# The feed-forward output of a hybrid decoder layer in three chunks of rows, two of them by a seven-product block scheme

## The chip, the cores and the metric

The kernel runs on one core of one Trainium2 chip. The metric is the device time of one execution in microseconds (us), the median of several runs. All arithmetic is fp32 in value: TensorE multiplies in a reduced fp32 format, so every operand is split into a high and a low part, and each block product is three products (high by high, high by low, low by high).

## The reference

One step of a one-layer decoder: 512 prompt rows and 8 sample rows (520 columns of a transposed activation), model width 1024, hidden width 2816 = 22 blocks of 128.

```python
h = x + Mixer(rmsnorm(x))            # retention, dilated attention, gates, w_o
a, b = split(rmsnorm(h) @ w_ffn_in, 2)
h = h + (silu(a) * b) @ w_ffn_out    # (520 x 2816) @ (2816 x 1024)
y = rmsnorm(h)
```

Beside `y`, the retention states and the key and value rows of the mixer are outputs.

## The kernel before

Activations lie transposed: 128 features on the partitions, the 520 columns in two halves of 260 (256 prompt and 4 sample columns, `HF`). Weights come from one array `wall` in the order of their use, as 194 subs; a sub is 128x1024, eight tiles of 128x128. `load_sub` has SyncE's queue load one (four buffers `raw`). `split_sub` has ScalarE write the high part `wh` of a whole sub, and two steps later VectorE the low part `wl` and the queue the load of the sub that takes the freed buffer; both parts have three buffers. A `product` takes one weight tile and runs six matmuls of 260 columns, three for each half. A `unit` runs `nk` products into one PSUM tile `pm` (two banks, one for each half; two such tiles exist) and asks for splits two subs ahead at every eighth product.

The program writes the order of every engine by hand. After each product `pump` takes one step of a queue of generators (`P`, `S`, `Q`), which issue the work beside the weights: scores, sample states, norms. `drain("P")` steps the generators until none is left, with nothing between.

The stages are, by the time of the profile: retention with its projections to about 430 us, then the output projections, attention, gates and `w_o` to about 946 us, then the feed forward. Its input (L1100 to L1121) makes 22 hidden blocks `U`, each by two units of 8 products: VectorE scales `fa` and `fb` (L1105, L1111), ScalarE takes Silu, VectorE multiplies (L1112), and the result is split into a high part (L1113) and a low part (L1114). After all 22, the output (L1194) makes eight column blocks `c` of the result by a unit of 22 products each, and `ev_f` adds them onto `hT` (L1191). The eighth is made one half after the other (L1200).

The final norm works by column block and half: `fin_T` transposes the block on TensorE into two of three PSUM banks `sp` (L212, three transposes), `fin_sq` has ScalarE sum the squares (`junk`, L1142 and L1144), `fin_g` has VectorE scale it (`yt` L1148, `ys` L1150). I call these three together a finish; there are 16. `gen_final` spreads two finishes over ten steps. `fin_out` makes the norm of a half from all its finishes (a power on GpSimd, L221), scales and stores.

```python
    for c in range(7):
        unit(NFF, usrc, lambda pm, c=c: ev_f(pm, c))
        push("P", gen_final(c))
```

Of the kernel before, what the change touches and what calls it, by code (L numbers as in the profile page):

```python
# [22 lines left out]
NFF = 22  # L23
NSUB = 194
GAMMA = [1.0 - 2.0 ** (-5.0 - h) for h in range(RH)]


@with_exitstack
def tile_hybrid_layer(
# [35 lines left out]
    def f32(ap):  # L65
        return ap.bitcast(F32)
# [70 lines left out]

    raw, split = {}, {}

    NRAW = 4  # L140

    def load_sub(s):
# [3 lines left out]

    def split_sub(s):
        if s >= NSUB or s in split:
            return
        r = raw.pop(s)  # L150
        h = wpool.tile([128, 1024], F32R, tag="wh", name=f"wh{s}")
        l = wpool.tile([128, 1024], F32R, tag="wl", name=f"wl{s}")
        A.activation(h, r, AF.Copy)  # L153
        split[s] = (h, l)

        def low():
            V.tensor_tensor(l, r, f32(h), op=ALU.subtract)  # L157
            load_sub(s + NRAW)

        later(2, low)  # L160

    tr = rp.tile([128, 2, C], F32, name="tr")
# [19 lines left out]
    def product(pm, n, k, nk, src, fs):  # L182
        h, l = split[n // 8]
        j = n % 8
        wh, wl = h[:, j * 128:(j + 1) * 128], l[:, j * 128:(j + 1) * 128]
        xh, xl = src(k)
        for w, x, first, last in ((wh, xh, k == 0, False), (wh, xl, False, False), (wl, xh, False, k == nk - 1)):
            for f in fs:
                PE.matmul(pm[:, f, :HF], w, x[:, f * HF:(f + 1) * HF], start=first, stop=last)  # L189

    def unit(nk, src, evac=None):
        pm = pmain.tile([128, 2, 512], F32, tag="pm", name="pm")
        for k in range(nk):
            n = pos[0]
            pos[0] += 1
            if n % 8 == 0:
                for s in range(3):
                    split_sub(n // 8 + s)
            product(pm, n, k, nk, src, (0, 1))
            pump()  # L200
        if evac:
            evac(pm[:, :, :HF])
        return pm[:, :, :HF]

    def sbank(name="sp"):
# [40 lines left out]

    for s in range(2):
        split[s] = tuple(wpool.tile([128, 1024], F32R, tag=t, name=f"{t}{s}") for t in ("wh", "wl"))

    def w_split(s, i):  # L250
        q = slice(512 * i, 512 * i + 512)
        (h, l), r = split[s], raw[s]
        A.activation(h[:, q], r[:, q], AF.Copy)
        V.tensor_tensor(l[:, q], r[:, q], f32(h[:, q]), op=ALU.subtract)

# [9 lines left out]
    for s in range(2):  # L265
        raw.pop(s)
        load_sub(NRAW + s)

# [72 lines left out]
    for h in range(RH):  # L341
# [245 lines left out]
        for which in ("q", "k"):  # L587
            e0, e1 = rot(which)
            if h == 0 and which == "q":
# [3 lines left out]
                for u, k in [(u, k) for k in range(4) for u in range(2)] + [(u, k) for u in range(2) for k in range(4, 8)]:  # L593
                    product(pms[u], 8 * u + k, k, 8, src, (0, 1))
                    if u and k == 4:
                        split_sub(2)
                    pump()
                    if k == 7:
                        (e0, e1)[u](pms[u][:, :, :HF])
# [442 lines left out]
    rs2 = hp.tile([128, C], F32, name="rs2")  # L1042
    fp = open_pool("fp", "right")
    X2 = bpool.tile([128, 16, C], F32R, tag="bx", name="X2")
    acc2 = fp.tile([128, C], F32, name="acc2")
# [48 lines left out]
    push("P", gen_norm2())  # L1094
    U = [None] * (2 * NFF)
    UA = bpool.tile([128, 16, C], F32R, tag="bg", name="UA")
    UB = fp.tile([128, 28, C], F32R, name="UB")
    for i in range(2 * NFF):
        U[i] = UA[:, i, :] if i < 16 else UB[:, i - 16, :]
    for i in range(NFF):  # L1100
# [50 lines left out]

    def gen_final(c):
        for _ in range(5):
            yield
        a = fin_T(c, 0)
        yield
        fin_sq(c, 0, *a)
        fin_g(c, 0, *a)
        yield
        yield  # L1160
        b = fin_T(c, 1)
        yield
        fin_sq(c, 1, *b)
        fin_g(c, 1, *b)

    def fin_out(f, sp, sp2):
        fin_sq(7, f, sp, sp2)
        s = fp.tile([128, 4], F32, tag="fs", bufs=2, name="fs")
        V.tensor_reduce(s[:, 0:2], ssp[:, 2 * f:2 * f + 2, :], AX.X, ALU.add)
        r = rstd_rows(fp, s[:, 0:2], 128, 2, D, "nf")  # L1170
        fin_g(7, f, sp, sp2)
        V.tensor_reduce(s[:4, 2:3], sss[:, f, :], AX.X, ALU.add)
# [12 lines left out]
    def usrc(k):  # L1185
        return U[k], U[NFF + k]

    def ev_f(pm, c, f=None):
        fs = slice(None) if f is None else slice(f, f + 1)
        h = halves(hT[:, c, :])[:, fs]  # L1190
        V.tensor_tensor(h, pm[:, fs], h, op=ALU.add)  # L1191
# [63 lines left out]
def _layout(np, i):  # L1255
# [14 lines left out]
    ffo = [j for c in range(NFF) for j in (c, NFF + c)]  # L1270
    flat = np.concatenate([x.reshape(-1, 128, 128) for x in
                           (w_in[seq], _tiles(f["w_pa"][0]), w_in[seq2], _tiles(f["w_pb"][0]), _tiles(f["w_o"][0]), ff[ffo],
                            _tiles(f["w_ffn_out"][0]))])
    wall = np.ascontiguousarray(flat.reshape(NSUB, 8, 128, 128).transpose(0, 2, 1, 3)).reshape(NSUB, 128, 1024)
# [24 lines left out]
```

## Time and profile before

| what | value |
|---|---|
| median of 3 runs | 1331.48 us (1330.41 to 1332.78) |
| the profiled execution, its own time | 1332.56 us |
| its span, first to last instruction | 1330.8 us |
| TensorE matmul busy | 1304.4 us, 98%, x10681 |
| VectorE busy | 662.5 us, 50% |
| ScalarE busy | 476.7 us, 36% |
| mean granted TensorE clock | 0.991 |

PE is TensorE's matmuls, PEld its weight loads, DVE VectorE, ACT ScalarE, POOL GpSimd, SP SyncE (SPq its queue). L189 is the line of `kernel.py` with the matmul of `product`; L157 and L153 are the low and the high part of the weight split. A busy PE is not PE at its peak: one matmul of 260 columns is recorded with 0.28 us, but starts 0.12 us after the one before it. In a stage without waits the start-to-start time is the cost.

### The profile page before, as it was taken

Reading aid. Unit: us, or ns where it says so; the run is one execution under the profiler, and the core shown is the slowest. Engines: PE = TensorE matmul, PEld = TensorE weight load, DVE = VectorE, ACT = ScalarE, POOL = GpSimd, SP = SyncE. Lnnn points to the kernel's source line nnn. Section 1 sums busy time; section 2 is a strip of 40 time slices with the busy share of each in tenths; the row PEclk is TensorE's granted clock in tenths of the full one; section 3 lists DMA queues with packets and bytes.
Section 4 is the critical chain, followed back from the end, with each engine's and each line's share of the span. In section 5 each row is a group of like instructions: output and inputs, shape, how many; then the busy total and the mean of one; then the engine's idle time right before and its main releaser. Section 6 shows DMA issues by size and latency. Waiting matters only on the chain.

```text
span 1330.8 us, 25131 instructions
## 1 busy us (share of the span) xinstructions
PE 1304.4 (98%) x10681; PEld 1273.4 (96%) x10681; DVE 662.5 (50%) x1271; ACT 476.7 (36%) x828; POOL 83.0 (6%) x69
## 2 busy tenths in 40 slices
PE   8999999999989999999999999999999999999997
PEld 7899999898889999999999999899999999999997
DVE  7867536746655432233545454376444444443323
ACT  4554334534453421143434343233222222222222
POOL 3601001001002000000000000030000000000000
PEclk9999999999899999999999999999999999999999
DMA  6267235646475233435555455634223332333221
GB/s 216 84 227 231 89 114 206 228 129 230 157 255 189 80 96 95 135 115 160 156 159 164 134 171 175 217 104 136 82 94 96 96 90 86 95 112 96 80 64 66
DMA packets 89777, 183.33 MB, mean 138 GB/s; under 512 B 12024, under 2 KB 33944, under 8 KB 89664
## 3 DMA queue, kind: packets, MB, share of 16 engines
q1 hardware_dynamic: 88944, 180.64, 43.2%
q8 instruction: 84, 1.38, 0.4%
q10 hardware_dynamic: 720, 1.07, 0.2%
q14 instruction: 29, 0.24, 0.1%
HBM read 155.70 MB, written 25.98 MB: 137 GB/s over the span
## 4 chain that ended last, share of the span: by engine, by line
PE 89%; DVE 4%; DMA 3%; ACT 1%; issue 1%; POOL 1%; SPq 1%; POOLq 0%; DVEq 0%; ACTq 0%
PE pm L189 78%; PE sp L212 3%; PE sp L442 2%; DMA vb<-vd 2%; PE sp L460 2%; DVE wl L157 1%; PE sp L394 1%; PE sp L852 1%; PE sp L802 1%; PE oacc L555 1%; PE sacc L997 1%; PE sp L791 0%; ACT wh L153 0%; DMA xb<-xT 0%; DVE X L313 0%
## 5 line engine op out<-in xcount | busy, mean ns | idle before, releaser
L189 PE MATMUL pm<-X,wh 128*128 128x260 f32 x4608 | 756.6, 286 | 3.9 <-DVE X L244 3.6
L189 PEld LDWEIGHTS pm<-X,wh 128*128 128x128 f32 x4608 | 636.7, 189 | 19.3 <-issue 8.2
L189 PE MATMUL pm<-X,wl 128*128 128x260 f32 x2304 | 465.0, 283 | 0.0
L189 PEld LDWEIGHTS pm<-X,wl 128*128 128x128 f32 x2304 | 356.3, 189 | 0.1
L157 DVE TENSOR_TENSOR wl<-raw,wh 128x1024 fp32r<-128x1024 f32 x192 | 236.6, 1233 | 169.9 <-ACT wh L153 169.2
L153 ACT ACTIVATE wh<-raw 128x1024 fp32r<-128x1024 f32 x192 | 201.7, 1051 | 174.2 <-PE pm L189 169.0
L189 PE MATMUL pm<-UB,wh 128*128 128x260 f32 x448 | 85.3, 282 | 0.0
L189 PE MATMUL pm<-GA,wh 128*128 128x260 f32 x512 | 82.2, 283 | 0.0
L189 PEld LDWEIGHTS pm<-GA,wh 128*128 128x128 f32 x512 | 70.1, 188 | 0.0
L189 PEld LDWEIGHTS pm<-UB,wh 128*128 128x128 f32 x448 | 67.2, 188 | 0.0
L221 POOL TENSOR_TENSOR r<-v,cst 128x4 f32<-128x4 f32 (+4 forms) x14 | 18.4, 1313 | 609.9 <-DVE v L219 609.8
L189 PE MATMUL pm<-UA,wh 128*128 128x260 f32 x256 | 55.3, 287 | 0.0
L510 ACT ACTIVATE kv<-vb,ks 128x512 f32<-128x512 f32 x64 | 44.0, 715 | 29.8 <-DMA vb<-vd 29.8
L545 DVE SCALAR_TENSOR_TENSOR st<-st,kv 128x512 f32<-128x512 f32 x64 | 45.9, 733 | 16.7 <-ACT kv L510 16.7
L189 PE MATMUL pm<-UA,wl 128*128 128x260 f32 x256 | 54.2, 283 | 0.0
L189 PE MATMUL pm<-GA,wl 128*128 128x260 f32 x256 | 51.6, 283 | 0.0
L1106 ACT ACTIVATE fa<-fa 128x520 f32<-128x520 f32 x22 | 14.0, 638 | 78.4 <-DVE fa L1105 78.4
L189 PE MATMUL pm<-M,wh 128*128 128x260 f32 x256 | 41.1, 282 | 0.0
L189 PEld LDWEIGHTS pm<-UA,wh 128*128 128x128 f32 x256 | 40.4, 188 | 0.3
L189 PEld LDWEIGHTS pm<-UA,wl 128*128 128x128 f32 x256 | 40.5, 188 | 0.0
L189 PEld LDWEIGHTS pm<-GA,wl 128*128 128x128 f32 x256 | 39.6, 188 | 0.0
L1111 DVE TENSOR_TENSOR fb<-pm,rs 128x520 f32<-128x520 f32 x22 | 15.4, 700 | 46.2 <-PE pm L189 46.2
(245 smaller groups left out, 1309.7 us busy)
## 6 DMA issues: line engine op xcount, KB each, us to landing
raw<-wall SPq DMA_DIRECT2D x192, 512.0 KB
st<-state SPq DMA_DIRECT2D x64, 256.0 KB
out<-st SPq DMA_DIRECT2D x64, 256.0 KB
area<-ck SPq DMA_DIRECT2D x24, 512.0 KB
vb<-vd SPq DMA_DIRECT2D x32, 256.0 KB
area<-qd SPq DMA_DIRECT2D x12, 512.0 KB
cb<-cd SPq DMA_DIRECT2D x4, 768.0 KB
xr<-xT SPq DMA_DIRECT2D x8, 260.0 KB
```

Source lines behind the costliest of these rows:

```text
L153: A.activation(h, r, AF.Copy)
L157: V.tensor_tensor(l, r, f32(h), op=ALU.subtract)
L189: PE.matmul(pm[:, f, :HF], w, x[:, f * HF:(f + 1) * HF], start=first, stop=last)
L212: PE.transpose(out, in_, ident[:n, :n])
L221: G_.tensor_tensor(r[:rows, :ncol], v[:rows, :ncol], mhalf[:rows].to_broadcast([rows, ncol]), op=ALU.pow)
L394: PE.matmul(sp[:, :T - i0], x[:, dt, jb * 128:(jb + 1) * 128], y[:, dt, i0:], start=i == 0, stop=i == len(mm) - 1)
L442: PE.matmul(sp[:, i0:], v[x][:, jb, c * 128:(c + 1) * 128], scs[y][:, SCO[jb]:SCO[jb] + T - i0], start=jb == 0 and x == y, stop=jb == 3 an ...
L460: PE.matmul(sp, kt[x][:, jb, dt * 128:(dt + 1) * 128], v[y][:, jb, :], start=jb == 0 and x == y, stop=jb == 3 and x == 1)
L510: A.activation(kvs[i][:, :DV], vbs[b], AF.Copy, scale=ks[:, dt, b:b + 1])
L545: V.scalar_tensor_tensor(sts[i], sts[i], GAMMA[h], kvs.pop(i)[:, :DV], op0=ALU.mult, op1=ALU.add)
L1106: A.activation(t, t, AF.Silu)
L1111: V.tensor_tensor(halves(t), pm, halves(rs2), op=ALU.mult)
```

## The change

The feed forward is cut along the hidden width into chunks of 8, 8 and 6 blocks. After the hidden blocks of a chunk (and the first one of the next) follows the share that this chunk adds to all eight column blocks.

For the first two chunks a share is made for two column blocks at once, `quad`. The weights there are a 2x2 arrangement of blocks (two column blocks by two interleaved sets of four hidden blocks), the activations one of 2x2 (two sets by two halves). Instead of eight block products there are seven, each of four weight tiles by one half, three matmuls a tile: 84 matmuls of 260 columns where eight products have 96. The operands are sums and differences. On the weight side `block_sum` has VectorE form them, in three additions over 2048 columns in all. On the activation side `right` forms four more halves from four, after every second hidden block, and splits seven halves in one instruction for each part. Three PSUM banks take the seven products. ScalarE copies the running content of a bank to SBUF after products 0, 1, 2 and 4 (`snap`), and VectorE adds banks and copies onto `hT` (`evac`, six additions).

Weights are now split in blocks of 512 columns, half a sub, in the whole kernel: six buffers for each part, and `advance` asks five blocks ahead at each new block.

The last chunk has six products a column block. Blocks 0 and 1 are made side by side, then 2 and 3, then blocks 4 to 7 for the first half of the columns and then for the second, from weights that stay in place. A `drain("P")` stands in the second half after the second product of block 5, ahead of `fin_out(0)`, and another one after the last product. `fin_out` comes after `fin_g` now.

```diff
+CHUNKS = ((0, 8), (8, 8), (16, 6))
+LAST = [(c, k) for k0 in (0, 4) for c in range(2) for k in range(k0, min(k0 + 4, 6))]
+LAST[8:] = [(0, 4), (1, 4), (0, 5), (1, 5)]
+QUADS = {s + 2 * i: 4 for s in (146, 170) for i in range(4)}
...
+    AHEAD = 5
...
-    def split_sub(s):
-        if s >= NSUB or s in split:
+    def left(b):
+        kind, s, j = blocks[b]
+        if kind == "p":
+            return raw[s][:, 512 * j:512 * j + 512]
+        w = 128 * QUADS[s]
+        t, i = ((s, 1), ("q", 0), (s + 1, 0), (s + 1, 1), ("q", 1), ("q", 0), (s, 0))[j]
+        return (qsum[s] if t == "q" else raw[t])[:, i * w:(i + 1) * w]
+
+    def block_sum(b):
+        kind, s, j = blocks[b]
+        if kind == "p":
             return
-        r = raw.pop(s)
-        h = wpool.tile([128, 1024], F32R, tag="wh", name=f"wh{s}")
-        l = wpool.tile([128, 1024], F32R, tag="wl", name=f"wl{s}")
+        w = 128 * QUADS[s]
+        if j == 1:
+            qsum[s] = home[0].tile([128, 1024], F32, tag="qq", name=f"qq{s}")
+            V.tensor_tensor(qsum[s][:, :2 * w].rearrange("p (i c) -> p i c", i=2),
+                            raw[s][:, :2 * w].rearrange("p (i c) -> p i c", i=2),
+                            raw[s + 1][:, :w][:, None, :].to_broadcast([128, 2, w]), op=ALU.add)
+        elif j == 2:
+            V.tensor_tensor(raw[s + 1][:, :w], raw[s][:, w:2 * w], qsum[s][:, :w], op=ALU.add)
+        elif j == 5:
+            V.tensor_tensor(qsum[s][:, :w], raw[s + 1][:, w:2 * w], raw[s + 1][:, :w], op=ALU.add)
+
+    def block_tiles(b):
+        w = 128 * QUADS[blocks[b][1]] if blocks[b][0] == "q" else 512
+        split[b] = tuple(wpool.tile([128, 512], F32R, tag=t, bufs=6, name=f"{t}{b}")[:, :w] for t in ("wh", "wl"))
+        return split[b]
+
+    def block_hi(b):
+        h, l = block_tiles(b)
+        r = left(b)
         A.activation(h, r, AF.Copy)
-        split[s] = (h, l)
 
         def low():
             V.tensor_tensor(l, r, f32(h), op=ALU.subtract)
-            load_sub(s + NRAW)
+            kind, s, j = blocks[b]
+            if kind == "p" and j == 1:
+                load_sub(s + NRAW)
+            elif kind == "q" and j == 6:
+                load_sub(s + NRAW)
+                load_sub(s + 1 + NRAW)
 
         later(2, low)
+
+    def advance(t):
+        while done["add"] < min(t + AHEAD + 2, len(blocks)):
+            b = done["add"]
+            done["add"] += 1
+            block_sum(b)
+        while done["hi"] < min(t + AHEAD + 1, len(blocks)):
+            b = done["hi"]
+            done["hi"] += 1
+            block_hi(b)
...
+    def begin(n):
+        if n % 4 == 0:
+            advance(bid[n // 8, n % 8 // 4])
+
...
-            if n % 8 == 0:
-                for s in range(3):
-                    split_sub(n // 8 + s)
+            begin(n)
...
+    SEVEN = ((0, 0), (1, 3), (0, 4), (2, 1), (0, 5), (1, 2), (0, 6))
+
+    def quad(xh, xl, snap, evac):
+
+        s = pos[0] // 8
+        pos[0] += 16
+        nkp = QUADS[s]
+        pm = pmain.tile([128, 2, 512], F32, tag="pm", name="pm")
+        out = [pm[:, 0, :HF], pm[:, 1, :HF], None]
+        begun = set()
+        for j, (bank, x) in enumerate(SEVEN):
+            advance(bid[s, 0] + j)
+            if bank == 2:
+                out[2] = abank("pc")[:, :HF]
+            h, l = split[bid[s, 0] + j]
+            for k in range(nkp):
+                ks = slice(k * 128, k * 128 + 128)
+                for w, r in ((h, xh), (h, xl), (l, xh)):
+                    PE.matmul(out[bank], w[:, ks], r[:, k, x, :], start=bank not in begun, stop=k == nkp - 1 and r is xh and w is l,
+                              skip_group_check=True)
+                    begun.add(bank)
+                if k % 2:
+                    pump()
+            if j in (0, 1, 2, 4):
+                A.activation(snap[(0, 3, 1, None, 2)[j]], out[bank], AF.Copy)
+            evac(j, out[bank])
+
+    def right(t, hi, lo):
+
+        V.tensor_tensor(t[:, 3, :], t[:, 0, :], t[:, 7, :], op=ALU.subtract)
+        V.scalar_tensor_tensor(t[:, 4, :], t[:, 2, :], -1.0, t[:, 3, :], op0=ALU.mult, op1=ALU.subtract)
+        V.tensor_tensor(t[:, 5, :], t[:, 2, :], t[:, 7, :], op=ALU.subtract)
+        V.scalar_tensor_tensor(t[:, 6, :], t[:, 4, :], -1.0, t[:, 1, :], op0=ALU.mult, op1=ALU.subtract)
+        A.activation(hi, t[:, 0:7, :], AF.Copy)
+        later(3, lambda: V.tensor_tensor(lo, t[:, 0:7, :], f32(hi), op=ALU.subtract))
...
+    def whole(i, t):
+        hi, lo = (halves(u[:, i - NP, :]) for u in (UHp, ULp))
+        A.activation(hi, t, AF.Copy)
+        later(2, lambda: V.tensor_tensor(lo, t, f32(hi), op=ALU.subtract))
+
+    def ffn_in(i):
...
         def ev_fb(pm, i=i, s=s):
             t = ftmp("fb")
             V.tensor_tensor(halves(t), pm, halves(rs2), op=ALU.mult)
-            V.tensor_tensor(t, t, s["a"], op=ALU.mult)
-            A.activation(U[i], t, AF.Copy)
-            later(2, lambda: V.tensor_tensor(U[NFF + i], t, f32(U[i]), op=ALU.subtract))
+            if i > NP:
+                V.tensor_tensor(t, t, s["a"], op=ALU.mult)
+                whole(i, halves(t))
+                return
+            V.tensor_tensor(UF[:, 1:3, :] if i % 2 else UF[:, 0::7, :], halves(t), halves(s["a"]), op=ALU.mult)
+            if i % 2:
+                k = i % 8 // 2
+                right(UF, UH4[:, k], UL4[:, k])
 
...
+    def ffn_out(c):
+        s12 = fp.tile([128, 2, HF], F32, tag="s12", bufs=2, name="s12")
+        s35 = fp.tile([128, 2, HF], F32, tag="s35", bufs=2, name="s35")
+        h1, h2 = halves(hT[:, c, :]), halves(hT[:, c + 1, :])
+
+        def evac(j, bank):
+            if j == 3:
+                V.tensor_tensor(h1[:, 0, :], bank, h1[:, 0, :], op=ALU.add)
+                later(1, lambda: V.tensor_tensor(h1, h1, s12, op=ALU.add))
+            elif j == 4:
+                later(1, lambda: V.tensor_tensor(s35[:, 0, :], s35[:, 0, :], s35[:, 1, :], op=ALU.add))
+            elif j == 5:
+                V.tensor_tensor(h1[:, 1, :], bank, h1[:, 1, :], op=ALU.add)
+                V.tensor_tensor(h2[:, 1, :], h2[:, 1, :], s35[:, 0, :], op=ALU.subtract)
+            elif j == 6:
+                V.tensor_tensor(h2[:, 0, :], h2[:, 0, :], bank, op=ALU.subtract)
+
+        quad(UH4, UL4, [s12[:, 0, :], s12[:, 1, :], s35[:, 0, :], s35[:, 1, :]], evac)
+
+    for (a, n), ahead in zip(CHUNKS, (1, 1, 0)):
+        if not ahead:
+            whole(NP, UF[:, 0::7, :])
+        for i in range(a and a + 1, a + n + ahead):
+            ffn_in(i)
+        if ahead:
+            for c in range(0, 8, 2):
+                ffn_out(c)
...
+    def gen_final(c, fs=(0, 1)):
+        for f in fs:
+            for _ in range(2 if f else 5):
+                yield
+            a = fin_T(c, f)
+            yield
+            fin_sq(c, f, *a)
+            fin_g(c, f, *a)
+            if f != fs[-1]:
+                yield
+
+    def fin_out(f):
...
-    for c in range(7):
-        unit(NFF, usrc, lambda pm, c=c: ev_f(pm, c))
+    nk = CHUNKS[2][1]
+    pms = [pmain.tile([128, 2, 512], F32, tag="pm", name="pm") for _ in range(2)]
+    base = pos[0]
+    for i, (c, k) in enumerate(LAST):
+        begin(base + i)
+        product(pms[c], base + i, k, nk, usrc, (0, 1))
+        pump()
+        if k == nk - 1:
+            ev_f(pms[c][:, :, :HF], c)
+            push("P", gen_final(c))
+    pos[0] = base + len(LAST)
+    for c in (2, 3):
+        unit(nk, usrc, lambda pm, c=c: ev_f(pm, c))
         push("P", gen_final(c))
     base = pos[0]
-    for s in range(base // 8, NSUB):
-        split_sub(s)
     for f in range(2):
-        pm = pmain.tile([128, 2, 512], F32, tag="pm", name="pm")
-        for k in range(NFF):
-            product(pm, base + k, k, NFF, usrc, (f,))
-            if f == 0 and k % 2:
-                pump()
-            if f == 1 and k == 2:
-                a = fin_T(7, 0)
-            if f == 1 and k == 5:
-                fin_out(0, *a)
-        ev_f(pm[:, :, :HF], 7, f)
+        for c in range(4, 8):
+            if c % 2 == 0:
+                pm = pmain.tile([128, 2, 512], F32, tag="pm", name="pm")
+            o = pm[:, c % 2:c % 2 + 1, :]
+            for k in range(nk):
+                n = base + (c - 4) * nk + k
+                if f == 0:
+                    begin(n)
+                h, l = split[bid[n // 8, n % 8 // 4]]
+                js = slice(n % 4 * 128, n % 4 * 128 + 128)
+                xh, xl = (u[:, f * HF:(f + 1) * HF] for u in usrc(k))
+                for i, (w, x) in enumerate(((h, xh), (h, xl), (l, xh))):
+                    PE.matmul(o[:, 0, :HF], w[:, js], x, start=k == 0 and i == 0, stop=k == nk - 1 and i == 2)
+                if k % 2:
+                    pump()
+                if f and c == 4 and k == 3:
+                    a = fin_T(7, 0)
+                if f and c == 4 and k == 5:
+                    fin_sq(7, 0, *a)
+                    fin_g(7, 0, *a)
+                if f and c == 5 and k == 1:
+                    drain("P")
+                    fin_out(0)
+            ev_f(o[:, :, :HF], c, f)
+            if c < 7:
+                push("P", gen_final(c, (f,)))
+    drain("P")
     a = fin_T(7, 1)
-    fin_out(1, *a)
+    fin_sq(7, 1, *a)
+    fin_g(7, 1, *a)
+    fin_out(1)
```

The order of the instructions, first on VectorE where the feed-forward output is made. Ahead, before the change: `wl` is the low part of a weight sub, the rest is the final norm and one addition onto `hT`.

```order
L157 TENSOR_TENSOR wl_13577<-raw_13322,wh_13576 128x1024
L157 TENSOR_TENSOR wl_13631<-raw_13402,wh_13630 128x1024
L1191 TENSOR_TENSOR hT<-pm,hT 128x520
L1148 TENSOR_TENSOR yt<-sp,gb 128x2x128
L1150 TENSOR_TENSOR ys<-sp,gb 4x128
L157 TENSOR_TENSOR wl_13692<-raw_13456,wh_13691 128x1024
```

And after the change, a part of one `quad`: `qq` and the new `raw` are sums of weights, `s` are the copies of banks, `pc` is the third bank.

```order
L179 TENSOR_TENSOR qq_12241<-raw_11963,raw_12025 128x1024
L198 TENSOR_TENSOR wl_12244<-raw_11963,wh_12243 128x512
L183 TENSOR_TENSOR raw_12025<-raw_11963,qq_12241 128x512
L198 TENSOR_TENSOR wl_12262<-qq_12241,wh_12261 128x512
L1239 TENSOR_TENSOR hT<-pc,hT 128x260
L1240 TENSOR_TENSOR hT<-hT,s_12200 128x520
L198 TENSOR_TENSOR wl_12280<-raw_12025,wh_12279 128x512
L1242 TENSOR_TENSOR s_12201<-s_12201 128x260
L198 TENSOR_TENSOR wl_12298<-raw_12025,wh_12297 128x512
L1244 TENSOR_TENSOR hT<-pm,hT 128x260
L1245 TENSOR_TENSOR hT<-hT,s_12201 128x260
L185 TENSOR_TENSOR qq_12241<-raw_12025 128x512
```

Between two low parts there now stand sums of weights and additions onto `hT`; one `quad` has seven low parts, three sums and six additions, 16 instructions.

On TensorE at the end of the program, before: each finish is a pair of rows onto `sp`, here with products before and behind it.

```order
L189 MATMUL pm_14441<-UA_10510,wl191_14201 128x260
L212 MATMUL sp_14451<-cst_90,hT_9984 128x128 x2
L212 MATMUL sp_14452<-cst_90,hT_9984 4x128
L189 MATMUL pm_14441<-UA_10510,wh191_14200 128x260
L189 MATMUL pm_14441<-UB_10511,wh191_14200 128x260
```

And after, from the second product of block 5 in the second half on, where the `drain("P")` stands.

```order
L1354 MATMUL pm_15236<-UH_11030,wl407_14985 128x260
L307 MATMUL sp_15288<-cst_90,hT_10472 128x128 x2
L307 MATMUL sp_15289<-cst_90,hT_10472 4x128
L307 MATMUL sp_15301<-cst_90,hT_10472 128x128 x2
L307 MATMUL sp_15302<-cst_90,hT_10472 4x128
L307 MATMUL sp_15314<-cst_90,hT_10472 128x128 x2
L307 MATMUL sp_15315<-cst_90,hT_10472 4x128
L307 MATMUL sp_15327<-cst_90,hT_10472 128x128 x2
L307 MATMUL sp_15328<-cst_90,hT_10472 4x128
L307 MATMUL sp_15340<-cst_90,hT_10472 128x128 x2
L307 MATMUL sp_15341<-cst_90,hT_10472 4x128
```

Two more such pairs follow, so that seven finishes stand in a row with no product between; behind them come the last 48 matmuls of the second half, with one finish after 30 of them and two after the last.

More of the change, by code (lines that the diff above doesn't have):

```diff
@@ L135, in finish @@
             step(name)
-    raw, split = {}, {}
+    raw, split, qsum = {}, {}, {}
+    blocks, bid = [], {}
+    for s_ in range(NSUB):
+        if s_ in QUADS:
+            bid[s_, 0] = len(blocks)
+            blocks += [("q", s_, j) for j in range(7)]
+        elif s_ - 1 not in QUADS:
+            bid[s_, 0], bid[s_, 1] = len(blocks), len(blocks) + 1
+            blocks += [("p", s_, 0), ("p", s_, 1)]
+    done = {"add": 0, "hi": 0}
+    home = []
     NRAW = 4
+    AHEAD = 5
     def load_sub(s):
@@ L182, in product @@
     def product(pm, n, k, nk, src, fs):
-        h, l = split[n // 8]
-        j = n % 8
+        h, l = split[bid[n // 8, n % 8 // 4]]
+        j = n % 4
         wh, wl = h[:, j * 128:(j + 1) * 128], l[:, j * 128:(j + 1) * 128]
@@ L245, in x0_split @@
                                op1=ALU.subtract)
-    for s in range(2):
-        split[s] = tuple(wpool.tile([128, 1024], F32R, tag=t, name=f"{t}{s}") for t in ("wh", "wl"))
+    for b in range(4):
+        block_tiles(b)
+    done["add"] = done["hi"] = 4
     def w_split(s, i):
[L251 to L254, printed above, removed]
+        (h, l), r = split[2 * s + i], left(2 * s + i)
+        A.activation(h, r, AF.Copy)
+        V.tensor_tensor(l, r, f32(h), op=ALU.subtract)
     for i in range(2):
@@ L265, in tile_hybrid_layer @@
     for s in range(2):
-        raw.pop(s)
         load_sub(NRAW + s)
@@ L595, in tile_hybrid_layer @@
                     if u and k == 4:
-                        split_sub(2)
+                        advance(0)
                     pump()
@@ L1043, in tile_hybrid_layer @@
     fp = open_pool("fp", "right")
+    home.append(fp)
     X2 = bpool.tile([128, 16, C], F32R, tag="bx", name="X2")
@@ L1094, in tile_hybrid_layer @@
     push("P", gen_norm2())
[L1095 to L1100, printed above, removed]
+    UH = bpool.tile([128, 28, HF], F32R, tag="bg", name="UH")
+    UL = fp.tile([128, 28, HF], F32R, name="UL")
+    UF = fp.tile([128, 8, HF], F32, name="UF")
+    UH4, UL4 = (u.rearrange("p (k x) c -> p k x c", x=7) for u in (UH, UL))
+    UHp, ULp = (u.rearrange("p (k f) c -> p k (f c)", f=2) for u in (UH, UL))
+    NP = CHUNKS[2][0]
+    def whole(i, t):
[3 more added lines that the diff above has]
+    def ffn_in(i):
         s = {}
@@ L1150, in fin_g @@
         V.tensor_tensor(ys[:, f, cs], sp2[:4, :128], gb[:4, cs], op=ALU.mult)
-    def gen_final(c):
-        for _ in range(5):
-            yield
[L1155 to L1167, printed above, removed]
+    def gen_final(c, fs=(0, 1)):
[3 more added lines that the diff above has]
+            a = fin_T(c, f)
+            yield
+            fin_sq(c, f, *a)
[3 more added lines that the diff above has]
+    def fin_out(f):
         s = fp.tile([128, 4], F32, tag="fs", bufs=2, name="fs")
@@ L1170, in fin_out @@
         r = rstd_rows(fp, s[:, 0:2], 128, 2, D, "nf")
-        fin_g(7, f, sp, sp2)
         V.tensor_reduce(s[:4, 2:3], sss[:, f, :], AX.X, ALU.add)
@@ L1185, in usrc @@
     def usrc(k):
-        return U[k], U[NFF + k]
+        return UHp[:, k, :], ULp[:, k, :]
     def ev_f(pm, c, f=None):
@@ L1190, in ev_f @@
         h = halves(hT[:, c, :])[:, fs]
-        V.tensor_tensor(h, pm[:, fs], h, op=ALU.add)
+        V.tensor_tensor(h, pm, h, op=ALU.add)
     pattern[:] = ["P"]
-    for c in range(7):
-        unit(NFF, usrc, lambda pm, c=c: ev_f(pm, c))
+    nk = CHUNKS[2][1]
[8 more added lines that the diff above has]
+            push("P", gen_final(c))
@@ L1269, in _layout, with quad @@
     ff = _tiles(f["w_ffn_in"][0])
[L1270 to L1273, printed above, removed]
+    ffi = ff[[j for c in range(NFF) for j in (c, NFF + c)]].reshape(NFF, 16, 128, 128)
+    fo = _tiles(f["w_ffn_out"][0])
+    def quad(w, c, a):
+        w = w[c:c + 2, a:a + 8].reshape(2, 4, 2, 128, 128)
+        return [w[1, :, 1], w[0, :, 0], w[1, :, 0], w[0, :, 1]]
+    parts = [w_in[seq], _tiles(f["w_pa"][0]), w_in[seq2], _tiles(f["w_pb"][0]), _tiles(f["w_o"][0])]
+    for (a, n), ahead in zip(CHUNKS, (1, 1, 0)):
+        parts.append(ffi[a and a + 1:a + n + ahead])
+        if ahead:
+            for c in range(0, 8, 2):
+                parts += quad(fo, c, a)
+        else:
+            parts += [fo[c, a + k] for c, k in LAST] + [fo[2:, a:]]
+    flat = np.concatenate([x.reshape(-1, 128, 128) for x in parts])
     wall = np.ascontiguousarray(flat.reshape(NSUB, 8, 128, 128).transpose(0, 2, 1, 3)).reshape(NSUB, 128, 1024)
```

1 line of the change is left out of this document (added).

## The prediction

> **What bounds the kernel now.** I read the chain of work that ended last first, then the busy time by stretches, then the waits, then the timeline of the last 20 us.
>
> ```profile
> PE 89%; DVE 4%; DMA 3%; ACT 1%; issue 1%; POOL 1%; SPq 1%; POOLq 0%; DVEq 0%; ACTq 0%
> 429.58 143.29 PE pm L189 x1194
> 946.10 263.93 PE pm L189 x2196
> 1226.81 2.16 PE pm L189 x18
> 1229.30 13.65 PE pm L189 x114
> 1243.28 2.15 PE pm L189 x18
> 1314.47 6.85 PE pm L189 x57
> ```
>
> The chain (start, length, what) is TensorE for 89% of the span. The feed forward is one piece: 2196 matmuls in 263.93 us, 0.1202 us each, with no wait in it. The last piece, where only one half is made, has the same rate (6.85/57 = 0.120). From 1226.81 to 1243.28 one column block of the output with two finishes takes 16.47 us; 132 matmuls are 15.86 us of it, so a finish among products costs TensorE 0.3 us.
>
> ```profile
> core 0: us, PE busy (x) PEld busy (x) DVE busy (x) ACT busy (x) POOL busy (x), PEclk, DMA share, GB/s
> 309.00:343.00 34.00, 29.03 (x195) 25.48 (x194) 27.52 (x45) 17.74 (x25) 1.40 (x1) 0.90 0.81 266
> 430.00:575.00 145.00, 145.00 (x1207) 144.77 (x1205) 52.69 (x74) 40.52 (x52) 0.94 (x2) 1.00 0.32 99
> 946.00:1211.00 265.00, 265.00 (x2207) 264.94 (x2207) 119.24 (x137) 72.84 (x96) 0.00 (x0) 1.00 0.31 93
> 1211.00:1311.00 100.00, 100.00 (x840) 99.70 (x839) 31.31 (x48) 27.11 (x90) 0.00 (x0) 1.00 0.23 68
> PE oacc L555 <- DVE y L526: 4.9, 2, 3.4
> PE sp L394 <- DVE pl L382: 2.2, 2, 1.2
> ```
>
> These are stretches of the span and then two rows of TensorE's waits (total, times, longest). From 430 us on TensorE is never out of work. In the retention part ahead of that it has gaps: in 309 to 343 us VectorE is busy for 27.5 of 34 us, and TensorE waits for it. So a matmul taken out of the feed forward is worth its full 0.120 us, as long as nothing that replaces it makes TensorE wait; and VectorE and ScalarE, at 31% and 27% in the output stretch, have room.
>
> **The matmuls.** Two chunks have 16 of 22 hidden blocks: 16 x 8 x 6 = 768 matmuls of 260 columns. Eight quads of 84 are 672. The 96 that go are worth 96 x 0.1202 = 11.5 us. The rest of the feed forward keeps its matmuls: 2112 in the input, 288 in the last chunk.
>
> **Inside a quad** (84 x 0.1202 = 10.1 us) I check each engine that TensorE waits for.
>
> ```profile
> L157 DVE TENSOR_TENSOR wl<-raw,wh x192: 1202/1226/2328, 22.6 to 1303.9; 128x1024 fp32r<-128x1024 f32 x192
> L254 DVE TENSOR_TENSOR wl<-raw,wh x4: 685/1240/1805, 5.3 to 15.4; 128x512 fp32r<-128x512 f32 x4
> L153 ACT ACTIVATE wh<-raw x192: 1039/1050/1064, 13.6 to 1302.8; 128x1024 fp32r<-128x1024 f32 x192
> L253 ACT ACTIVATE wh<-raw x4: 613/624/634, 4.5 to 10.9; 128x512 fp32r<-128x512 f32 x4
> L1191 DVE TENSOR_TENSOR hT<-pm,hT x9: 429/699/700, 1205.7 to 1321.3; 128x520 f32<-128x520 f32 x7, 128x260 f32<-128x260 f32 x2
> 1312.27 0.42 DVE L1148 TENSOR_TENSOR yt<-sp,gb 128x256 f32<-128x256 f32 x1 [1.89 <-ACT junk L1142]
> 1312.61 0.27 DVE L1150 TENSOR_TENSOR ys<-sp,gb 4x128 f32<-4x128 f32 x1
> 1312.77 0.29 PE L189 MATMUL pm<-UB,wl 128*128 128x260 f32 x1
> 1313.10 0.43 DVE L1191 TENSOR_TENSOR hT<-pm,hT 128x260 f32<-128x260 f32 x1 [0.22 <-PE pm L189]
> ```
>
> The first five rows give the least, median and largest duration in ns. VectorE has seven low parts of 512 columns (0.685), three sums (1.226 + 2 x 0.685) and six additions (five of 260 columns at no more than 0.429, one of 520 at 0.700): 4.8 + 2.6 + 2.8 = 10.2 us by full durations. But a second instruction starts 0.34 us after a first of 0.42, an overlap of 0.08; with 16 of these it is 9.0 us. So VectorE is nearly full for ten microseconds, with bounds of 89 and 101% of TensorE's time. Even the upper end lets it fall behind by 0.1 us a quad, and low parts are asked for five blocks (7.2 us) ahead, so I cost it at nothing. The cover is that lead.
>
> ScalarE has seven high parts (0.624) and four copies of 260 columns. A copy lies between the 128 columns of a `junk` (0.273, below) and a high part of 512; on the line between, 0.39 us. That is 5.9 us of 10.1. A tighter place is the bank: product 0 fills bank 0, the copy must have read it before product 2 writes there, and between lies product 1 alone, 12 x 0.120 = 1.44 us. The reader of a finished bank starts 0.33 us after its last matmul did (1312.77 to 1313.10), 0.21 after the next one may start. 0.21 + 0.39 = 0.60, and with one high part in the way 1.22 us. It fits; I cost it at nothing, with 0.2 us to spare.
>
> On the activation side `right` is four additions (at most 1.7 us) and a split of 1820 columns, 1.8 us on ScalarE and 2.1 on VectorE by the slopes of the rows above. It runs after the second of two hidden blocks, while the next block's 96 matmuls (11.5 us) hide it; VectorE is at 45% there. SyncE's queue keeps its order and bytes; at the quads it loads two subs at once, 1 MB every 10 us or about 105 GB/s, where the first stretch above moved 266. Only the load of the norm's weights moves behind the quads, some 17 products (12 us) ahead of its use. Cost nothing.
>
> **Splits by halves** touch the whole kernel: for each sub VectorE gets 2 x 685 - 1226 = 144 ns more and ScalarE 2 x 624 - 1050 = 198. From 430 us on this lies beside free time. In the retention part there are 54 subs that were split whole (4 heads of 12 column blocks and 8 more, less the first two), so VectorE gets 7.8 us more over 430 us; only what falls into the stretches where TensorE waits for VectorE counts, a fifth or so of them. The smaller pieces also let a waiting instruction through earlier, and blocks are asked for 20 products ahead, where it was 16. Between 7.8 lost and 3.5 gained (half of the 7.1 that TensorE waits for `y` and `pl` above) I take 0.
>
> **The last chunk.** Here is one finish among products, and the norm behind it.
>
> ```profile
> 1313.86 0.28 PE L189 MATMUL pm<-UA,wl 128*128 128x260 f32 x1
> 1313.98 0.49 PE L212 MATMUL sp<-cst,hT 128*128 128x128 f32 x3
> 1314.23 0.37 PE L189 MATMUL pm<-UA,wh 128*128 128x260 f32 x1
> 1314.46 0.28 ACT L1142 ACTIVATE junk<-sp 128x128 f32<-128x128 f32 x1 [1.99 <-PE sp L212]
> 1315.13 0.18 ACT L1144 ACTIVATION_READ_ACCUMULATOR junk<-sp 4x1 f32 x1
> 1311.61 0.28 ACT L1142 ACTIVATE junk<-sp 128x128 f32<-128x128 f32 x1 [1.64 <-PE sp L212]
> 1315.12 0.17 DVE L1169 TENSOR_REDUCE fs<-ssp 128x2 f32<-128x16 f32 x1 [1.59 <-ACT junk L1142]
> 1315.57 1.29 POOL L221 TENSOR_TENSOR r<-v,cst 128x2 f32<-128x2 f32 x2 [372.57 <-DVE v L219]
> 1317.12 0.73 DVE L1182 TENSOR_SCALAR ys<-ys,r 4x1024 f32<-4x1024 f32 x1
> L1142 ACT ACTIVATE junk<-sp 128x128 f32<-128x128 f32 x32 | 8.6, 273 | 31.6 <-PE sp L212 31.6
> ```
>
> A finish starts ScalarE 0.48 us after the first transpose and holds it for 0.85 (1314.46 to 1315.31); VectorE's `yt` starts 0.66 after ScalarE did (1311.61 to 1312.27) and `ys` ends at 1312.88, 1.75 us after the transposes. Seven finishes stand in the row that `drain` makes. Each wants two of three banks: the third is free at once, the other one only when the `yt` of the finish ahead has ended, and the next one after `ys`. Drawn out with these times, the finishes follow each other at 0.92 us, and the next product can start 0.9 us after the seventh began: 6 x 0.92 + 0.9 = 6.4 us in place of 7 x 0.3. That costs 4.1 us. If ScalarE alone set the pace (0.85) with no wait for the last `yt`, it would be 3.3; if each waited for all of the one ahead (1.75), 8.7. I take 4.1, since the third bank lets transposes run ahead.
>
> Smaller things: block 2 wants the banks of block 0 only 6 matmuls (0.72) after they are full, and the addition ends 0.21 + 0.70 after: 0.2 us. Two finishes with 6 matmuls between, where a bank is free 1.6 us after the first began: 0.3 us. At the end two finishes come where one was, and `yt` and `ys` stand ahead of the sum: 0.8 us.
>
> `fin_out(0)` now waits behind the seventh finish. From its first transpose to the end of `ys` scaling before is 3.87 us (1313.98 to 1317.85); `fin_g` ahead of the sum adds 0.55, and behind all this on VectorE waits the addition of block 5 (0.43), for which a finish waits after 30 matmuls: 4.95 us after the seventh finish began, where TensorE comes there after 0.9 + 3.6 = 4.5. That is 0.45 us.
>
> ```profile
> 394.17 1.91 PE L555 MATMUL oacc<-y,om 128*32 128x512 f32 x2 [3.40 <-DVE y L526]
> 394.00:396.00 2.00, 1.83 (x2) 0.18 (x2) 2.00 (x5) 1.97 (x3) 0.00 (x0) 0.50 0.77 255
> 396.00:398.00 2.00, 2.00 (x9) 1.90 (x9) 1.36 (x3) 0.00 (x0) 0.00 (x0) 0.50 0.64 161
> 398.00:400.00 2.00, 2.00 (x10) 1.81 (x9) 0.00 (x0) 0.72 (x1) 0.00 (x0) 0.59 1.04 394
> 400.00:404.00 4.00, 4.00 (x30) 3.87 (x29) 1.95 (x3) 1.89 (x3) 0.00 (x0) 1.00 1.00 343
> ```
>
> The clock may add to it. After a wait of 3.40 us in the retention part TensorE was granted half its clock for some 5.5 us (0.50, 0.50, 0.59, then 1.00). If the row of finishes counts as such a wait, the products behind lose up to 2.7 us, 0.45 of it in the wait just named. Bounds 0.45 and 2.7; I take 1.2, as TensorE is not idle there. [...]
>
> **The sum.** -11.5 + 4.1 + 0.2 + 0.3 + 0.8 + 1.2 = -4.9 us. Against the profiled execution's own 1332.56 that is 1327.7; the median of the runs shown lies 1.1 lower, so 1326.6.
>
> **Rivals.**
>
> First, the saving arrives almost whole: the finishes run at ScalarE's pace beside each other and the halves smooth the retention part by 1 to 2 us. For it speaks that VectorE's waits there are short; against it, that only three banks hold the finishes. -11.5 + 3.3 + 0.2 + 0.8 + 0.45 - 2 = -8.8: 1322.7.
>
> Second, on the other side: the halves are paid in the retention part. Each sub's 144 ns on VectorE falls on the chain, because TensorE there waits for what VectorE does last. All 54 subs give 7.8 us, so +2.9: 1334.4. It is slower than before once more than 63% of them count (4.9/7.8). For it speaks the stretch at 27.5 of 34 us and that ScalarE's part grows as well; against it, that the two kinds of wait on VectorE quoted there come to 7.1 us in four places, so that few subs can sit in them. [...]
>
> Third, banks: the copies come late in the quads, because a high part waits for a sum of weights and the copy behind it in ScalarE's order. If each of the three returns to bank 0 lost a high part's 0.62 us, it is 1.9 us a quad and 15 us in all: 1341.6. It needs VectorE more than 1 us behind, and the sums above let it be that for single blocks only.
>
> **How the numbers follow.** A measurement of this kernel tells about 0.2% (2.7 us) from no change, so faster is under 1328.8 and slower over 1334.1. The forecast with its bounds (the row of finishes mostly 3.3 to 6, the clock 0.45 to 2.7, one or two microseconds either way in the retention part) runs from 1324 to 1332 and gets 0.60, of which 0.43 lies below 1328.8. The first rival gets 0.20, all faster. The second gets 0.13, half of it within 0.2%; the third 0.07, slower. That gives faster 0.63, same 0.24, slower 0.13. The range 1321.5 to 1333.0 reaches into the first and second rivals; it leaves out the third and the far end of the second, and a little below.
>
> **What would show it.** 3072 matmuls in the feed forward where 3168 were, and quads of 10.1 us with no wait of TensorE: right. Seven finishes in 6 to 7 us near the end with TensorE waiting for `yt` or `ys`: right; under 4 us, the first rival. The retention part ending (the first piece of over 100 us of products) more than 3 us later than at 429.58: the second rival. Waits of TensorE on ScalarE's copies in the quads: the third. What I can most easily have wrong is the row of finishes, which is drawn from one finish at a time, and the retention part, where small shifts of the order decide who waits.

## The result, and the profile after

The changed kernel takes 1346.33 us (median of four runs, 1344.79 to 1348.70), where the kernel before, run beside it, takes 1331.24: a ratio of 1.0114, 95% interval 1.0096 to 1.0131. It is 1.1% slower, and 13 us above the upper end of the predicted range. The profiled execution took 1344.79 us with a span of 1343.0; before it was 1332.56 with 1330.8, so the traces have 12.2 us to explain. Two executions in the experiments below, one of the kernel before (3194.92 us) and one with half blocks alone (3093.53 us), are left out of the ranges and ratios.

The chain of work after, in the same view as before: first the shares by engine, then the long pieces.

```profile
PE 88%; DVE 4%; DMA 3%; ACT 2%; issue 1%; POOL 1%; SPq 0%; DVEq 0%; ACTq 0%
422.12 143.29 PE pm L245 x1194
938.63 93.81 PE pm L245 x780
1034.36 1.72 PE pm L282 x12
...
1047.45 1.72 PE pm L282 x12
...
1060.53 1.72 PE pm L282 x12
...
1084.79 92.25 PE pm L245 x768
1229.37 65.61 PE pm L245 x546
```

TensorE still carries the chain, but the one piece of 2196 matmuls has become long pieces with the quads in fragments between them. The same product of two quads (L282) recurs after 13.09 and 13.08 us; 84 matmuls without a wait would be 10.1. From the first quad (1032.45) to the end of the last (1229.37) are 196.92 us; less the 92.25 of input products between, the eight quads take 104.7, or 13.08 each.

The waits of TensorE over the whole span (total, times, longest) name what fills the difference.

```profile
PE pm L282 <- ACT s L288: 11.4, 24, 0.5
PE pm L282 <- DVE hT L1244: 4.2, 8, 0.5
PE pm L245 <- DVE X L339: 3.6, 3, 1.5
PE sp L307 <- DVE yt L1285: 2.8, 7, 0.9
PE oacc L649 <- DVE y L620: 2.3, 2, 1.4
...
PE pm L1354 <- DVE hT L1323: 1.3, 3, 0.6
```

There are 32 waits in eight quads, four in each: 24 for ScalarE's copy of a bank, eight for VectorE's addition. Their 15.6 us are idle time counted from the recorded end of a matmul; counted from start to start the loss is larger. The timeline at one of them, with the idle time and what ended it in brackets:

```profile
1059.65 0.29 PE L282 MATMUL pm<-UL,wh 128*128 128x260 f32 x1
...
1059.78 0.28 PE L282 MATMUL pm<-UH,wl 128*128 128x260 f32 x1
1060.09 0.39 ACT L288 ACTIVATE s<-pm 128x260 f32<-128x260 f32 x1 [0.88 <-PE pm L282]
...
1060.53 0.39 PE L282 MATMUL pm<-UH,wh 128*128 128x260 f32 x1 [0.48 <-ACT s L288]
...
1060.76 0.28 PE L282 MATMUL pm<-UL,wh 128*128 128x260 f32 x1
```

The matmul at 1059.78 is the last of product 0, which fills bank 0. ScalarE is idle, begins the copy of bank 0 at once and ends it at 1060.48. The matmul at 1060.53 is the first of product 1, which writes bank 1. Nothing reads bank 1, and still it starts only when the copy of bank 0 has ended. From one start to the next are 0.75 us where products follow at 0.12, and the one after it comes 0.23 later: 0.74 us lost in all. Four of these are 3.0 us a quad, and 24 us in eight.

By pieces of the trace, after less before: the part up to the long piece at 422.12 (429.58 before) -7.5; 96 matmuls -11.5; eight quads 8 x (13.08 - 10.09) = +24.0; the rest, nearly all of it behind the last quad, +7.2. Together +12.2.

### The profile page after: what moved, and what is told of

The parts are those of the page before. It is cut to its first block, busy times and chain, and to the rows that moved or that the text cites. A ratio compares the mean times of both kernels' runs of the same rounds, so it can differ in the third digit from the quotient of the medians.

```text
span 1343.0 us, 25698 instructions
## 1 busy us (share of the span) xinstructions
PE 1299.2 (97%) x10585; PEld 1259.3 (94%) x10585; DVE 757.6 (56%) x1586; ACT 535.4 (40%) x1068; POOL 83.5 (6%) x69
## 4 chain that ended last, share of the span: by engine, by line
PE 88%; DVE 4%; DMA 3%; ACT 2%; issue 1%; POOL 1%; SPq 0%; DVEq 0%; ACTq 0%
PE pm L245 69%; PE pm L282 6%; PE sp L307 2%; DMA vb<-vd 2%; PE sp L536 2%; PE sp L554 2%; PE sp L946 1%; PE pm L1354 1%; PE sp L488 1%; PE pc L282 1%; ACT s L288 1%; DVE wl L198 1%; PE sp L896 1%; PE oacc L649 1%; PE sacc L1091 1%
## 5 line engine op out<-in xcount | busy, mean ns | idle before, releaser
L198 DVE TENSOR_TENSOR wl<-raw,wh 128x512 fp32r<-128x512 f32 x384 | 275.0, 720 | 218.5 <-ACT wh L195 216.5
L195 ACT ACTIVATE wh<-raw 128x512 fp32r<-128x512 f32 x384 | 237.9, 625 | 242.6 <-PE pm L245 182.3
L282 PE MATMUL pm<-UH,wh 128*128 128x260 f32 x192 | 57.6, 300 | 15.6 <-ACT s L288 11.4
L282 PEld LDWEIGHTS pm<-UH,wh 128*128 128x128 f32 x192 | 36.1, 188 | 22.3 <-ACT s L288 16.4
L316 POOL TENSOR_TENSOR r<-v,cst 128x4 f32<-128x4 f32 (+4 forms) x14 | 17.6, 1260 | 621.3 <-DVE fs L1304 399.9
L282 PE MATMUL pm<-UL,wh 128*128 128x260 f32 x192 | 54.2, 282 | 0.0
L282 PE MATMUL pm<-UH,wl 128*128 128x260 f32 x192 | 54.1, 282 | 0.0
L639 DVE SCALAR_TENSOR_TENSOR st<-st,kv 128x512 f32<-128x512 f32 x64 | 45.3, 712 | 12.3 <-ACT kv L604 11.4
L282 PEld LDWEIGHTS pm<-UL,wh 128*128 128x128 f32 x192 | 36.1, 188 | 0.0
L282 PEld LDWEIGHTS pm<-UH,wl 128*128 128x128 f32 x192 | 36.1, 188 | 0.0
L245 PEld LDWEIGHTS pm<-M,wh 128*128 128x128 f32 x256 | 35.1, 188 | 0.0
```

The lines of the kernel that those rows point to most:

```text
L282: PE.matmul(out[bank], w[:, ks], r[:, k, x, :], start=bank not in begun, stop=k == nkp - 1 and r is xh and w is l, skip_group_check=True)
L316: G_.tensor_tensor(r[:rows, :ncol], v[:rows, :ncol], mhalf[:rows].to_broadcast([rows, ncol]), op=ALU.pow)
L639: V.scalar_tensor_tensor(sts[i], sts[i], GAMMA[h], kvs.pop(i)[:, :DV], op0=ALU.mult, op1=ALU.add)
```

## The experiments

My theory after the result: bank 0 and bank 1 of a quad are two halves of one tile `pm`, and the program makes a write to either half wait for what reads the other. The rivals: the copies themselves, or VectorE at nine tenths, are what a quad waits for; and the gain ahead of 430 us does not come from the half blocks.

**The banks as tiles of their own.** The quad's two banks come from the pool of single banks; nothing else is changed.

```
-        pm = pmain.tile([128, 2, 512], F32, tag="pm", name="pm")
-        out = [pm[:, 0, :HF], pm[:, 1, :HF], None]
+        b1, b0 = sbank("pb"), sbank("pa")
+        out = [b0[:, :HF], b1[:, :HF], None]
```

> The changed kernel with one edit: the two banks that a quad shares in one PSUM tile become two PSUM tiles of a bank each (taken from the three banks of the norm, which are idle then). Theory A, the wait belongs to the tile: a product must not start while ScalarE or VectorE reads the other bank of the same tile, 0.73 us at each of four handovers in eight quads, 23.6 us. With two tiles those 32 waits go, a quad takes 10.1 to 10.3 us in place of 13.1, and the time is 1346.3 - 23.6 = 1322.7 us (1321 to 1325). Rival B, the copies are late, ScalarE being held up by high parts and sums: bank 0 comes back after one product as before, the waits stay on products 2, 4 and 6, 0.5 us or more each, and the time stays above 1334.

Measured: 1324.10 us (1323.57 to 1327.02), 0.9944 of before [0.9926, 0.9961]. The chain in the quads and two quads as stretches (engine by engine as busy time and count, then the granted clock):

```profile
1033.86 1.44 PE pa L282 x12
1035.29 1.44 PE pb L282 x12
1036.73 1.45 PE pa L282 x12
1038.18 1.44 PE pc L282 x12
...
1033.86:1043.95 10.09, 10.09 (x86) 10.09 (x86) 10.02 (x19) 5.54 (x11) 0.00 (x0) 1.00 0.36 106
1043.95:1054.04 10.09, 10.09 (x86) 10.09 (x86) 9.16 (x18) 5.53 (x11) 0.00 (x0) 1.00 0.34 106
```

A quad is 10.09 us and TensorE never waits in it, with the same copies, sums and additions as before the edit. So the copies are not late and VectorE is not the bound, though it is busy 10.02 and 9.16 us of 10.09. Nor does it cost anything to read one bank while another is filled: `pa` is copied here while `pb` is filled, at 1.44 us a product. Only the tile that the banks belong to was at fault, and that was 24 us in the quads. The median fell by 22.2, because in this trace the part ahead of the long piece is 1.4 us longer and the part behind the quads 1.3 longer.

**Half blocks alone.** The kernel before with its weights split and asked for by halves, 20 products ahead, and nothing else of the change: `product` takes `split[bid[n // 8, n % 8 // 4]]`, and `advance` stands where `split_sub` stood, with no quads in the list of blocks.

> The kernel before with one part of the change: weights split in blocks of 512 columns, six buffers, five blocks ahead. No chunks, no quads, the output and the norm as before. The changed kernel reached the end of the retention part 7.5 us earlier. Theory A, the halves do that (waiting work on ScalarE and VectorE gets through between them, TensorE's waits are shorter and its clock is not halved): 1331.2 - 7.5 = 1323.7 us (1321 to 1326), the first long piece of products starting near 422. Rival B, it has another cause (the phase of the clock, chance of an execution): 1331 within 1.5, or slower by up to 7.8 if the fixed cost of the pieces shows.

Measured: 1325.11 us (1323.25 to 1327.88), 0.9947 [0.9931, 0.9964]. The long piece starts at 422.63, where it started at 429.58 before and at 422.12 after the whole change. The half blocks alone give the gain in the retention part.

**The end rearranged.** The changed kernel with a tile for each column block of the last part, finishes spread singly between products, and `fin_out(0)` behind the last of them, so that no row of seven is left.

```
-            if c % 2 == 0:
-                pm = pmain.tile([128, 2, 512], F32, tag="pm", name="pm")
-            o = pm[:, c % 2:c % 2 + 1, :]
+            pm = pmain.tile([128, 2, 512], F32, tag="pm", name="pm")
+            o = pm[:, 0:1, :]
...
-                if f and c == 5 and k == 1:
-                    drain("P")
-                    fin_out(0)
+                if f and c == 5 and k == 3:
+                    finish("P", last0)
+                    fin_out(0)
```

> The changed kernel with its last chunk rearranged: each column block of the halves has a PSUM tile of its own, block 0 ends two products ahead of block 1, the finishes are spread (two steps each, no idle steps), no row of them; the norm of the first half comes one product later. The quads keep their shared tile. Theory A: the row of seven finishes (6.2 us where 2.3 would do), four waits of 0.7 us on a shared tile and 0.8 us of waits of finishes go: 1346.3 - 7 = 1339 us (1338 to 1341). Rival B, the finishes are bound by ScalarE and VectorE wherever they stand and push the norm behind the end: 1344 to 1346.

Measured: 1340.69 us (1339.41 to 1341.32), 1.0062 [1.0046, 1.0079]: 5.6 below the whole change. By the traces the part from the long piece to the end of the span went from 920.9 us to 914.2, 6.7 less; the part ahead of it was 1.3 longer in this execution.

**Both edits together.**

> Both edits, a PSUM tile for each bank of a quad and the rearranged last chunk. Theory A, the two are independent: 1346.3 - 23.6 - 7 = 1315.7 us (1313 to 1318). Rival B, VectorE is now the limit of the quads (10.2 us of work by full durations in 10.1 us) and carries its lag into the last chunk: 1319 to 1325.

Measured: 1314.95 us (1312.54 to 1319.76), 0.9874 [0.9855, 0.9894]. It is 17.6 us faster than before and 31 faster than the change as made. TensorE's waits from 900 us on are two kinds, 1.2 us together, and VectorE at 89% in four quads costs nothing:

```profile
PE sp L307 <- DVE hT L1322: 0.7, 2, 0.5
PE sp L307 <- DVE yt L1285: 0.5, 1, 0.5
1033.23:1073.58 40.35, 40.35 (x339) 40.35 (x338) 35.97 (x64) 22.23 (x45) 0.00 (x0) 1.00 0.38 119
```

**Eight products for seven.** The same kernel with plain block products in the first two chunks.

```
-QUADS = {s + 2 * i: 4 for s in (146, 170) for i in range(4)}
+QUADS = {}
...
-        quad(UH4, UL4, [s12[:, 0, :], s12[:, 1, :], s35[:, 0, :], s35[:, 1, :]], evac)
+        for cc in (c, c + 1):
+            h = halves(hT[:, cc, :])
+            unit(8, lambda k: (UHp[:, (a + k) % 14, :], ULp[:, (a + k) % 14, :]),
+                 lambda pm, h=h: V.tensor_tensor(h, pm, h, op=ALU.add))
```

> The kernel of the run before (banks as tiles, rearranged end) with eight plain products of a share instead of seven: chunks, half blocks and end stay, the sums of weights and activations, the copies and the quads go, 96 matmuls come back. If a quad whose banks are tiles of their own costs nothing but its 84 matmuls, this adds 96 x 0.1202 = 11.5 us to 1314.95: 1326.5, with no wait of TensorE in the output shares, and the retention part as it was. If the sums, copies and the nearly full VectorE still cost something in a quad, the difference is smaller: at 0.7 us a quad left over, 6 us, 1321.

Measured: 1327.36 us (1327.09 to 1328.32), 0.996 of before [0.9946, 0.9973] and 12.4 us above the kernel with seven. The chain shows where the long piece of the feed forward's input starts, first in the kernel with eight, then in the one with seven:

```profile
941.12 345.26 PE pm L245 x2874
```

```profile
939.42 93.81 PE pm L245 x780
```

From there to the end of the span are 1326.4 - 941.1 = 385.3 and 1313.2 - 939.4 = 373.8: 11.5 us, the 96 matmuls at 0.120 and nothing else. The remaining 1.7 us of the span lie ahead of the feed forward, in code that the two kernels share.

**Half blocks with the old lead.** The kernel with half blocks alone, asked for 16 products ahead as before the change.

```
-    AHEAD = 5
+    AHEAD = 4
```

> The kernel before with blocks of weights split by halves, as in the earlier run that gave 1325.11, but asked for 16 products ahead as in the kernel before, not 20. If the gain of the retention part comes from the smaller pieces, which let a waiting instruction through earlier, it stays: 1324 to 1326.5, the long piece of products from about 422.6 us. If it comes from the longer lead, it goes: 1331 to 1334, the long piece from about 429.6 us, with the waits of over 3 us for VectorE's y back.

Measured: 1328.40 us (1327.07 to 1328.92), 0.9965 [0.9953, 0.9978], between the two forecasts. The long piece starts at 422.93, as with the longer lead: the pieces, not the lead, give the retention gain. But behind it are three waits that neither the kernel before nor the longer lead has:

```profile
PE pm L240 <- DVE sT L993: 3.1, 3, 1.3
943.01 263.91 PE pm L240 x2196
```

The feed forward's long piece starts at 943.01, where it started at 939.13 with the longer lead. So the lead is worth 3 to 4 us as well, in a place that I had not looked at; why half blocks need it there and whole ones did not stays open.

## Why the prediction was wrong, step by step

**The step that failed is "Inside a quad", costed at nothing.** I reasoned by bank: between two writes to bank 0 lies product 1, 1.44 us, and the copy ends 0.60 after the next matmul may start. The times were right: the copy took 0.39 us, as estimated, and ended 0.58 after the next product could have started (1059.90 to 1060.48). What I did not ask is what the next product waits for. `quad` takes one tile `pm` with two banks, and the order is kept by tile (32 waits in the quads with the shared tile, none with a tile for each bank), so product 1 stands behind the copy of product 0 although it writes another bank. The cover that I named, product 1, was itself what waited. It was 0.74 us for each change of bank inside the tile, four times a quad (0 to 1, 1 to 2, 4 to 5, 5 to 6); around product 3, whose `pc` is a tile of its own, there is none. That is 24.0 us where 0 was put, and it makes more than the whole miss: 1326.6 + 24.0 - 7 is 1344, against 1346.3.

In the feed forward before the change every tile was filled whole and then read whole, so no row of its trace had a price for this, and I took the absence of a wait for its cost. The third rival had the right place (banks, copies, TensorE waiting for them; 15 us, 1341.6) with the wrong mechanism: it needed ScalarE to be late, and ScalarE was idle 0.88 us ahead of the copy.

**The matmuls**: -11.5, right to a tenth of a microsecond by the run with eight products.

**VectorE in a quad**: forecast 9.0 to 10.2 of 10.1 us, measured 9.16 and 10.02 in the run with banks of their own and 9.0 as the mean of four quads in the run with both edits; ScalarE 5.9, measured 5.5. It costs nothing, as said.

**Splits by halves**: put at 0 between +7.8 and -3.5. The retention part gained 7.5, and the half blocks alone show 7.0 there. I counted the 144 ns that VectorE pays for each sub and bounded the gain by half of two waits. Of those, the wait for `y` fell from 4.9 to 2.3 and its longest case from 3.4 to 1.4. I bounded the gain by these two waits and left out the other waits and the clock. One stretch before, then after, then with half blocks alone:

```profile
345.00:430.00 85.00, 81.60 (x614) 74.99 (x613) 47.66 (x86) 38.51 (x61) 8.60 (x7) 0.96 0.60 200
```

```profile
345.00:430.00 85.00, 81.69 (x632) 75.88 (x631) 48.45 (x99) 38.64 (x67) 9.51 (x8) 1.00 0.62 203
```

```profile
345.00:430.00 85.00, 83.45 (x647) 77.61 (x646) 50.41 (x104) 40.78 (x71) 9.51 (x8) 1.00 0.63 205
```

TensorE is granted 0.96 before and 1.00 after, which is 3.4 us of 85 if all of it is lost time. How the gain divides between waits and clock differs from run to run. The table has the start of the long piece, the sum of TensorE's rows of waits ahead of 430 us, and the granted clock in five stretches of 85 us, from 5 us on.

| kernel | long piece | waits, us | granted clock |
|---|---|---|---|
| before | 429.58 | 17.1 | 0.98 1.00 1.00 0.96 0.96 |
| after | 422.12 | 15.1 | 1.00 1.00 1.00 0.98 1.00 |
| half blocks alone | 422.63 | 12.3 | 0.96 1.00 1.00 0.98 1.00 |
| half blocks, old lead | 422.93 | 10.9 | 0.94 1.00 1.00 0.96 1.00 |

After the change the waits are only 2.0 us shorter, and the clock that is missing to 1.00 costs 6.8 us less (0.10 x 85 = 8.5 before, 0.02 x 85 = 1.7 after, an estimate). With half blocks alone it is 4.8 of waits and 3.4 of clock. With the old lead it is 6.2 of waits and nothing of clock (8.5 in both), and the long piece still starts 6.7 us earlier than before. These sums lie between 0.5 us below and 1.3 above the gains, as the clock is printed to hundredths. So the gain does not need the clock; why one execution has shorter waits and another a better clock stays open. In the seven traces with half blocks the long piece starts between 422.12 and 424.62 us, so the 7.5 is the upper end of what they give. The second rival, which had the halves cost time here, was wrong in sign; the first, which had them smooth this part by 1 to 2 us, had the sign right and the size too small.

**The row of seven finishes**: 6.4 us forecast; the first transposes began at 1320.40, the next product at 1326.61, 6.2 us. The mechanism was right: TensorE waits five times for `yt` in the row, and the finishes follow each other at 0.93 us (ScalarE's first reads, 1320.88 to 1326.46, in six steps) where 0.92 was drawn. The forecast's subtraction has a slip: 6.4 less 7 x 0.3 is 4.3, not 4.1; that the measured 6.2 less 2.1 is 4.1 is luck.

```profile
1320.40 0.71 PE L307 MATMUL sp<-cst,hT 128*128 128x128 f32 x5
...
1322.02 1.47 PE L307 MATMUL sp<-cst,hT 128*4 128x128 f32 x6 [0.91 <-DVE yt L1285]
...
1324.73 0.63 PE L307 MATMUL sp<-cst,hT 128*4 128x128 f32 x3 [0.23 <-DVE yt L1285]
...
1326.61 0.37 PE L1354 MATMUL pm<-UH,wh 128*128 128x260 f32 x1
```

The addition of block 5 held a finish for about 0.47 us at 1330.76 (forecast 0.45, but its terms 3.87, 0.55 and 0.43 add up to 4.85 and not 4.95, which leaves 0.35). Block 2 lost about 0.2, as forecast. The clock term (1.2 with this 0.45 in it) was too big for this trace: the seven microseconds behind the row ran at full clock.

```profile
1326.60:1333.60 7.00, 6.70 (x55) 6.37 (x55) 4.01 (x15) 2.92 (x14) 1.26 (x2) 1.00 0.43 155
```

In the run with the banks in tiles of their own the same row is 6.2 us long as well, and there TensorE has half its clock for three microseconds behind it:

```profile
1297.85:1304.05 6.20, 3.93 (x23) 1.88 (x22) 3.64 (x12) 5.47 (x37) 0.00 (x0) 0.99 0.00 1
1304.05:1307.20 3.15, 3.15 (x15) 3.15 (x16) 2.08 (x10) 1.67 (x8) 1.26 (x2) 0.50 0.03 5
```

The first 30 matmuls behind the row start within 5.01 us there and within 3.56 in the changed kernel, so the clock cost 1.45 us, inside the bounds of 0.45 and 2.7. The forecast left open whether the row counts as a wait like the one of 3.40 us in the trace of before, behind which the clock was 0.50. Measured were both: 0.50 behind the row in the run with banks of their own, 1.00 in the changed kernel. The gaps in the two rows are alike, the longest 0.91 us in both; what decides between them no run shows.

The end, put at +0.8, came to 0: from the start of the last product's last matmul to the end of the span are 9.8 us in both kernels. In its place stand three waits of the quads' kind, since column blocks 4 and 5, and 6 and 7, share a tile (the waits at L1354 above, about 0.6 us each). So the terms of the end were 6.6 in sum and 7.2 as measured; that they lie so near is partly luck.

**What of the sum held.** With the banks in tiles of their own and all else as made, the kernel measured 1324.10 us, inside the range and faster than before as forecast. Its span is 9.1 us below that of before: -6.0 in the part up to the long piece (423.56), -11.5 for the matmuls, nothing in the quads and +8.5 behind them. There it has the half clock behind the row (1.45) and a fourth wait at L1354 (about 0.4), but not the wait of 0.47 for block 5. The forecast had 0, -11.5, 0 and +6.6. That the kernel comes so near to it is partly luck: without the 6.0 in the retention part, which was put at 0, it would take 1330 us, inside the range but not clearly faster than before.

## What to carry to other kernels

Ask of every buffer not when its bytes come free but what unit the program keeps order by: two banks in one tile are one buffer (a quad took 13.08 us with them, 10.09 with a tile for each bank), and a scheme that fills one half while the other is read must take two tiles. Where the kernel before never overlapped a reader and a writer inside a tile, its trace has no row for the price, and no wait seen there is not a cost of nothing; bound it by the full handover (here last matmul to first matmul through a copy, 0.75 us) times the count. And a saving of products is worth its full time once nothing waits, 11.5 us of 11.5 in this kernel, so a result far off that sum is a wait that can be found and taken away: here an edit of two lines gave back 22 us.

## What the runs showed that I had not expected

Splitting the same work into pieces of half the size made a part that was short of VectorE (busy for 27.5 of the 34 us from 309 to 343 before the change) faster by 5 to 7.5 us in seven traces, though each sub costs VectorE 158 ns more (two low parts of 692 ns for one of 1226, medians). In the trace after, the longest wait for `y` fell from 3.40 us to 1.44, and the half clock behind the 3.40 us wait (0.50 for some 5.5 us in the trace of before) was gone. In that trace the better clock is the larger part of the gain; with the old lead the clock over the whole part was no better than before, and TensorE's waits are 6.2 us shorter in sum.

The same row of seven finishes, with gaps alike (the longest 0.91 us in both), was followed by half the clock in one execution (0.50) and by the full clock in another (1.00). A clock seen in one trace is not yet a property of the kernel.
